# Eight of the convolution's 31 taps as products with diagonal matrices

## The chip, the cores and the metric

One core of a Trainium2 chip runs the kernel. The metric is the device time of one execution in microseconds (us). Engines are named as in the profile: PE is TensorE (PEld its weight loads), DVE is VectorE, ACT is ScalarE, POOL is GpSimd, SP is SyncE, whose queue issues nearly all loads.

## The reference, cut to what matters

A trunk of two layers over 256 tokens of 1024 features. Each layer mixes tokens, then applies a feed-forward block (dense in layer 0, the best two of eight experts in layer 1) and an embedding gate. The part that the change touches is the causal depthwise convolution of the mixer, 31 taps wide, over 512 channels:

```
v = a * jax.nn.sigmoid(gate)
vp = jnp.pad(v, ((0, 0), (CONV_WIDTH - 1, 0), (0, 0)))
y = lax.conv_general_dilated(vp, w_dw[:, None, :], ..., feature_group_count=D_CONV) + b_dw
y = jax.nn.silu(layer_norm(y, g_ln, b_ln));  return y @ w_pw
```

Each channel has its own 31 weights, so with channels on the partitions a tap is "shifted row times one weight per partition, added up". The conv result and the result of a pooling group are concatenated and multiplied by an output projection.

## The kernel before, in words

Everything is float32. Wide products use weights split into a high and a low part in a faster format: three matmuls (L347 high by high, L351 high by low, L352 low by high) for one product. Weights named in `DIRECT` are used whole (L344, L580, L573, L622): such a float32 product is one call in the code and two instructions, each with its own weight load, in the trace. Weight tiles come from one pool of 19 slots; SP issues a load when a slot comes free. ACT casts the high part (L146) and DVE forms the low part (L161).

The engines' orders are written out by hand: `mixer` issues the instructions in program order, and each engine runs its own in that order. The 512 channels are two blocks `b` of two 128-channel columns `i`. For a block, `gate` and `value` project the input (tiles `ps_g`, `ps_v`; each `h` is half of the tokens; 24 instructions for one block and half), ACT takes the sigmoid (L518), DVE multiplies (L523), PE transposes (`turn`, tile `tr`) and a copy puts the result into `vT[b]`, channels on partitions, with room to its left for the shifted reads.

`taps` then emits the taps. With `DT` = 20 and 21 for the two blocks, taps 0 to DT-1 go to DVE (L487 the first, L490 the others, each 128x256, adding into tile `yc`). The other 11 or 10 are made by ACT as products (L492, L495) and summed by POOL into `part` (L498, 128x512). DVE adds `part` to `yc` at the end (L513). The taps of block 0 start when `vT[0]` is there, with the products for block 1 between them: `gate(1,0)`, taps 0 to 4, `value(1,0)`, `gate(1,1)`, more taps, `turn(1,0)`, `value(1,1)`, the remaining taps. Then come the pooling group (`ps_u`, 24 instructions, `turn(1,1)`, 24 more; `ps_d`, `ps_y`), block 1's taps, the first half of the output projection (`ps_o`, L344, four groups of 4 products = 8 instructions, order (c,h) = (0,0), (0,1), (1,0), (1,1)), and the transposes of `yc` (L601, tile `ps_t`), which need all taps. After the third group, by `TS_AT = (1, 0)`, those transposes are put into PE's order. Then follow the layer norm of the conv result (L387 to L609), its transposes (L335), the pointwise product (L622) and the rest of the output projection.

PSUM tiles from `mmt` rotate over four banks, so a tile waits for the reader of the fourth tile before it. In layer 1 the mixer begins while the last input half is still being made: inside `value(0,0)` the function `late` transposes it, ACT casts it (L320, `xH`) and DVE forms its low part (L321, `xL`) for `gate(0,1)`.

Of the kernel before, what the change touches and what calls it, by code (L numbers as in the profile page):

```python
# [9 lines left out]
F32 = mybir.dt.float32  # L10
F32R = mybir.dt.float32r
I32 = mybir.dt.int32
AF = mybir.ActivationFunctionType
ALU = mybir.AluOpType
# [3 lines left out]
P = 128  # L18
D = 1024
S = 256  # L20
# [4 lines left out]
TAPS = 31  # L25
NG = 4
# [8 lines left out]
ND = len(DENSE_CHUNKS)  # L35
SLOTS = 19
HL_START, HL_PRE, HL_FIRST, HL_SECOND, HL_MOE = 8, 12, 8, 6, 10
WO0 = 0
DIRECT = ("pw0", "pw1", "wo00", "wo01")
DT = ((20, 21), (20, 21))  # L40
MORE_AT = 53
NPROD = 8
WARM = 16
WARM1 = 7
GB = 3
# [2 lines left out]
WU_EARLY = 2  # L48
GK = 5
PH = 1  # L50
AHEAD = ((0, 1), (1, 1))
RT = 8
WU_POOL = 3
KP = 5
# [1 line left out]
GL = 6  # L56
END = ((0, 256), (256, 256))
GAINS_AT, PLE_AT = 5, 3
TS_AT = (1, 0)
TEMPS_START, TEMPS_MIX, TEMPS_FFN, TEMPS_MOE, TEMPS_END, TEMPS_GATE = 6, 5, 4, 1, 4, 7  # L60

V_CW, V_CB, V_PS = 0, 124, 128
# [134 lines left out]
def trunk(ctx: ExitStack, tc: tile.TileContext, a: dict, out: bass.AP):  # L197
    nc = tc.nc
# [9 lines left out]
    def acc(name, k=None):  # L208

        if k is None:  # L210
            k = at[0] % 4
            at[0] += 1
        return pacc.tile([P, 512], F32, tag=f"acc{k}", name=name)

    def mmt(name):
        return pmm.tile([P, 512], F32, tag="mm", name=name)

    def tl(tag, shape, dt=F32):
        return ap.tile([P] + shape, dt, tag=tag, name=tag)

    W = Weights(nc, wp)
# [67 lines left out]
    vec = cp.tile([P, L, NV], F32, name="vec")  # L289
# [3 lines left out]
    ident = con[:, C_ID:C_ID + P]  # L293
# [20 lines left out]
    def table(func):  # L314

        nc.scalar.activation(dummy, neghalf, func)
# [25 lines left out]
    def mm(ps, x, it, cols, start, stop):  # L342
        if it["direct"]:
            nc.tensor.matmul(ps, x.f, it["F"][cols], start=start, stop=stop)  # L344
        else:
            wh, wl = it["H"][cols], it["L"][cols]
            nc.tensor.matmul(ps, x.h, wh, start=start, stop=False)  # L347
            if x.l is None:
                nc.tensor.matmul(ps, x.h, wl, start=False, stop=stop)  # L349
            else:  # L350
                nc.tensor.matmul(ps, x.h, wl, start=False, stop=False)  # L351
                nc.tensor.matmul(ps, x.l, wh, start=False, stop=stop)  # L352
# [3 lines left out]
    def proj(ids, ps, x, k0=0, first=True, last=True, free=False, also=None):  # L356

        at = k0
        for n, i in enumerate(ids):
            it = W.get(i)  # L360
            for j in range(it["k"]):
                mm(ps[:, :it["n"]], x[:, at, :], it, (ALL, j), first and n == 0 and j == 0,
                   last and n == len(ids) - 1 and j == it["k"] - 1)
                if also:
                    also(at)
                at += 1
            if free:
                W.done(i)
# [27 lines left out]
    def gains(l, name, n, q=nc.gpsimd, r=None):  # L396
        r = W.temp([2, n]) if r is None else r
        for i, s in enumerate("gb"):
            q.dma_start(r[:, i], a[f"{name}_{s}"][l:l + 1, :].to_broadcast([P, n]))
        return r[:, 0], r[:, 1]  # L400
# [46 lines left out]
    def mixer_loads(l):  # L447

        vs = W.temp([4, 32 + S])
        nc.gpsimd.memset(vs[:, :, 0:32], 0.0)  # L450
        q = nc.sync if l == 0 else nc.gpsimd
        pool = W.temp([16, P])
        mw = pool[:, :12].rearrange("p (a b) t -> p a (b t)", a=NG)
        plw = pool[:, 12:]
        for i in range(2):
            q.dma_start(mw[:, 2 * i:2 * i + 2], a["mw"][i])
        q.dma_start(plw.rearrange("p a b -> p (a b)"), a["w_small"][l, :, 2048:2560])
        cgb = gains(l, "conv_ln", NCONV, q, pd := W.temp([4, NCONV]))
        pd = pd[:, 2:].rearrange("p a (b t) -> p (a b) t", b=2)
        if l == 0:  # L460
            for h in range(2):
                q.dma_start(xr[h], a["x"][h])
        return vs, mw, plw, cgb, pd, W.temp([8, S])

    def mixer(l, xT, xr, late, loads):

        v = [tl(f"s{h}", [512]) for h in range(2)]
        vs, mw, plw, cgb, pd, prod = loads
        vT = [vs[:, 2 * b:2 * b + 2] for b in range(2)]
        yc = tl("yc", [4, S])  # L470
        vb = [[v[h][:, b * 256:(b + 1) * 256] for h in range(2)] for b in range(2)]


        if WO0:
            catP = Split(tl("cat", [NG, S], F32R), prod[:, 4:].bitcast(F32R))
        else:
            catP = Split(None, None, tl("cat", [NG, S]))
        part = [tl(f"gH{b}", [2, S]) for b in range(2)]
        count = [0]

        def tap(b, i, t):
            dt = DT[l][b]
            ct = 2 * b + i
            w1 = vec[:, l, V_CW + ct * TAPS + t:V_CW + ct * TAPS + t + 1]
            src = vT[b][:, i, 2 + t:2 + t + S]
            if t == 0:
                nc.vector.tensor_scalar(yc[:, ct], src, w1, vec[:, l, V_CB + ct:V_CB + ct + 1],  # L487
                                        op0=ALU.mult, op1=ALU.add)
            elif t < dt:
                nc.vector.scalar_tensor_tensor(yc[:, ct], src, w1, yc[:, ct], op0=ALU.mult, op1=ALU.add)  # L490
            elif t == dt:
                nc.scalar.activation(part[b][:, i], src, AF.Copy, scale=w1)  # L492
            else:
                p = prod[:, count[0] % (NPROD // 2) * 2:][:, :2]
                nc.scalar.activation(p[:, i], src, AF.Copy, scale=w1)  # L495
                if i:
                    count[0] += 1
                    nc.gpsimd.tensor_tensor(part[b], part[b], p, op=ALU.add)  # L498

        def taps(b, lo=0, hi=None):  # L500
            dt = DT[l][b]
            hi = hi or dt
            n = TAPS - dt
            by = lambda t: min(n, t * n // dt + (min(t, AHEAD[l][b])))
            for t in range(lo, hi):
                for i in range(2):
                    tap(b, i, t)
                for u_ in range(by(t), by(t + 1)):
                    for i in range(2):
                        tap(b, i, dt + u_)  # L510
            if b and hi == dt:
                for b_ in range(2):
                    nc.vector.tensor_add(yc[:, 2 * b_:2 * b_ + 2], yc[:, 2 * b_:2 * b_ + 2], part[b_])  # L513

        def gate(b, h, between=None):
            pg = acc("ps_g")
            proj(W.names[f"wg{b}{l}"], pg, xT[h], free=h == 1, also=lambda k: k == GB and between and between())
            nc.scalar.activation(vb[b][h], pg[:, :256], AF.Sigmoid)  # L518

        def value(b, h, between=None):  # L520
            pv = acc("ps_v")
            proj(W.names[f"wv{b}{l}"], pv, xT[h], free=h == 1, also=lambda k: k == GB and between and between())
            nc.vector.tensor_mul(vb[b][h], pv[:, :256], vb[b][h])  # L523
# [3 lines left out]
            copy(vT[b][:, :, 32 + h * P:32 + (h + 1) * P], transposes(vb[b][h], 2))  # L527

        W.temps = TEMPS_MIX

        gate(0, 0)
        if l == 0:
# [13 lines left out]
        W.prepare(f"wu{l}", WU_POOL)  # L546
        W.prepare(f"wu{l}", 4, "later")
        taps(0, 0, 5)
        value(1, 0)
        gate(1, 1)  # L550
        taps(0, 5, RT)
# [2 lines left out]
        turn(1, 0)  # L554
        table(AF.Silu)
        value(1, 1)
        taps(0, 12)

        u = [tl(f"g{h}", [512]) for h in range(2)]
        ps = [acc("ps_u") for h in range(2)]  # L560
        ids = W.names[f"wu{l}"]
# [9 lines left out]
        ps = [mmt("ps_d") for g in range(NG)]  # L571
# [6 lines left out]
        for g in range(NG):  # L578
            ps = mmt("ps_y")
            nc.tensor.matmul(ps[:, :S], plw[:, g, :], pd[:, g, :], start=True, stop=True)  # L580
            w = vec[:, l, V_PS + g:V_PS + g + 1]
            nc.scalar.activation((catP.h if WO0 else catP.f)[:, g], ps[:, :S], AF.Copy, scale=w)
            if WO0: nc.vector.scalar_tensor_tensor(catP.l[:, g], ps[:, :S], w, catP.h[:, g].bitcast(F32),
                                           op0=ALU.mult, op1=ALU.subtract)
        taps(1, T1[4])
        W.prepare(f"wo1{l}", None, "later")
        gb = gains(l, "ln1", D, nc.scalar)
# [3 lines left out]
        mix = [[acc("ps_o") for c in range(2)] for h in range(2)]  # L591
        ts = []
        ids = W.names[f"wo0{l}"]
        for c in range(2):
            for h in range(2):
                proj(ids[2 * c:2 * c + 2] if WO0 else ids[c:c + 1], mix[h][c], catP[:, :, h * P:(h + 1) * P], last=False, free=h == 1)
                if (c, h) == TS_AT:
                    for j in range(2):
                        t = mmt("ps_t")
                        for ct in range(4):  # L600
                            nc.tensor.transpose(t[:, ct * P:(ct + 1) * P], yc[:, ct, j * P:(j + 1) * P], ident)  # L601
                        ts.append(t)
# [31 lines left out]
        ps = pointwise(sT[0], lambda: turned(1))  # L634
# [573 lines left out]
    loads = mixer_loads(0)  # L1208
    for l in range(L):
        r = mixer(l, xT, xr, late, loads)  # L1210
        if l % 2 == 0:
            xT, late, ple, loads = dense(l, xr, *r)
# [97 lines left out]
```

## Time and profile before

| what | value |
|---|---|
| time, median of 3 runs (lowest to highest) | 1396.31 us (1393.35 to 1396.6) |
| profiled execution: own time, span | 1394.91 us, 1393.1 us |
| PE busy | 1302.4 us, 93% |
| DVE busy | 1194.2 us, 86% |
| ACT busy | 936.8 us, 67% |
| POOL busy | 92.1 us, of it the sums of taps (L498) 66.1 us in 38 instructions |
| DVE taps L490 | 156 instructions, 91.8 us, mean 660 ns by the grouped page, 467 to 1518 ns each |
| granted PE clock, mean | 0.969 |

The span is from the first to the last instruction; the execution's own time is 1.8 us longer. A busy share is a mean over stages with different limits, so the two mixers (about 31 to 120 us and 345 to 440 us) have to be read by themselves. [...]

### The profile page before, as it was taken

The numbers are of one execution on the slowest core, as the hardware profiler recorded it, in microseconds if no ns is written. First come the engines' busy times: TensorE is split into PE (matmuls) and PEld (weight loads), VectorE is DVE, ScalarE is ACT, GpSimd is POOL, SyncE is SP. The second block draws the span as 40 slices with busy tenths as digits, with TensorE's granted clock in tenths as the row PEclk, the third lists the DMA queues.
The fourth block names the chain that finished last, engine by engine and source line by source line (L and its number), as shares of the span: only waits on it lengthen the run. The fifth ranks groups of instructions, "written<-read, shape, count | busy, mean of one in ns | idle before, by whom it ended". The sixth has DMA issues, their size and how long they took to land. (4 is left out here: it accounts for less than half of the span.)

```text
span 1393.1 us, 16896 instructions
## 1 busy us (share of the span) xinstructions
PE 1302.4 (93%) x6186; PEld 1067.9 (77%) x6186; DVE 1194.2 (86%) x1082; ACT 936.8 (67%) x883; POOL 92.1 (7%) x71
## 2 busy tenths in 40 slices
PE   6769999999868999999999999999999999999777
PEld 5638888888737788878888887788887888888556
DVE  3997844457868698999999999999999999999885
ACT  4543744435444577887888887888888788898652
POOL 0330000001470200000000000000000000000000
PEclk8889999999989899999999999999999999999998
DMA  9334755526545399999999999999999999999850
GB/s 381 129 112 166 264 187 196 192 69 242 219 167 187 109 363 364 421 421 376 403 420 408 400 421 387 390 421 405 400 421 404 376 420 414 388 378 420 353 211 30
DMA packets 62171, 433.08 MB, mean 311 GB/s; under 512 B 6960, under 2 KB 7472, under 8 KB 11008
## 3 DMA queue, kind: packets, MB, share of 16 engines
q1 hardware_dynamic: 60336, 425.60, 77.3%
q0 software_dynamic: 1168, 4.23, 0.9%
q10 hardware_dynamic: 576, 2.10, 0.5%
q8 instruction: 50, 0.82, 0.2%
q14 instruction: 41, 0.34, 0.1%
HBM read 430.85 MB, written 1.05 MB: 310 GB/s over the span
## 5 line engine op out<-in xcount | busy, mean ns | idle before, releaser
L161 DVE TENSOR_TENSOR w<-w 128x2048 fp32r<-128x2048 f32 (+1 forms) x460 | 891.4, 1985 | 53.0 <-ACT w L146 46.7
L146 ACT CAST w<-w 128x2048 fp32r<-128x2048 f32 (+1 forms) x460 | 750.7, 1672 | 134.8 <-PE p L351 42.7
L347 PE MATMUL p<-w,xH 128*128 128x512 f32 (+1 forms) x1096 | 434.0, 396 | 9.0 <-DVEq L1039 6.0
L352 PE MATMUL p<-w,xL 128*128 128x512 f32 (+1 forms) x648 | 250.9, 387 | 1.3 <-DVE xL L321 1.3
L351 PE MATMUL p<-w,xH 128*128 128x512 f32 (+1 forms) x648 | 250.4, 386 | 0.4 <-DVE w L161 0.4
L347 PEld LDWEIGHTS p<-w,xH 128*128 128x128 f32 x1096 | 207.7, 190 | 51.3 <-issue 6.7
L347 PE MATMUL y<-w,gH 128*128 128x512 f32 x448 | 176.2, 393 | 3.0 <-DVE gH L382 2.3
L349 PE MATMUL p<-w,xH 128*128 128x512 f32 x448 | 176.1, 393 | 0.0
L352 PEld LDWEIGHTS p<-w,xL 128*128 128x128 f32 x648 | 122.6, 189 | 26.6 <-DVE xL L321 1.8
L351 PEld LDWEIGHTS p<-w,xH 128*128 128x128 f32 x648 | 122.7, 189 | 24.6 <-DVE w L161 1.3
L347 PEld LDWEIGHTS y<-w,gH 128*128 128x128 f32 x448 | 84.6, 189 | 21.4 <-DVE gH L382 3.0
L349 PEld LDWEIGHTS p<-w,xH 128*128 128x128 f32 x448 | 85.1, 190 | 17.0
L490 DVE SCALAR_TENSOR_TENSOR yc<-w,vec,yc 128x256 f32<-128x256 f32 x156 | 91.8, 660 | 0.0
L349 PE MATMUL y<-w,gH 128*128 128x512 f32 x224 | 88.3, 394 | 1.9 <-DVE w L161 1.9
L352 PE MATMUL y<-w,gL 128*128 128x512 f32 x224 | 87.4, 390 | 1.2 <-DVE gL L321 1.2
L351 PE MATMUL y<-w,gH 128*128 128x512 f32 x224 | 87.3, 390 | 0.0
L498 POOL TENSOR_TENSOR gH<-gH,w 128x512 f32<-128x512 f32 x38 | 66.1, 1738 | 108.5 <-ACT w L495 106.0
L429 POOL DMA_DIRECT2D w<-in_pT x2 | 1.2, 580 | 960.7 <-DVE w L161 802.4
L652 ACT ACTIVATE s<-p 128x512 f32<-128x512 f32 (+1 forms) x69 | 41.1, 598 | 28.0 <-PE p L352 28.0
L321 DVE TENSOR_TENSOR gL<-tr,gH 128x512 fp32r<-128x512 f32 x38 | 25.6, 683 | 32.7 <-ACT gH L320 32.7
L320 ACT CAST gH<-tr 128x512 fp32r<-128x512 f32 x38 | 21.8, 586 | 43.6 <-PE tr L335 43.0
L349 PEld LDWEIGHTS y<-w,gH 128*128 128x128 f32 x224 | 42.5, 190 | 11.0 <-DVE w L161 2.3
(223 smaller groups left out, 1483.3 us busy)
## 6 DMA issues: line engine op xcount, KB each, us to landing
w<-in_exp_w SPq DMA_DIRECT2D x336, 1024.0 KB, 8.8
w<-in_dense_w SPq DMA_DIRECT2D x33, 1024.0 KB, 5.0
w<-in_w_out SPq DMA_DIRECT2D x8, 1024.0 KB, 6.7
w<-in_ple_gate_w SPq DMA_DIRECT2D x8, 1024.0 KB, 5.5
w<-in_w_gv SPq DMA_DIRECT2D x6, 1024.0 KB, 7.3
w<-in_w_u SPq DMA_DIRECT2D x4, 1024.0 KB, 10.2
w<-in_w_gv SPq DMA_DIRECT2D x4, 512.0 KB, 6.7
w<-in_w_small SPq DMA_DIRECT2D x2, 1024.0 KB, 10.5
```

The source lines that it names most:

```text
L146: nc.scalar.copy(h, w)
L161: engine.tensor_tensor(l, w, h.bitcast(F32), op=ALU.subtract)
L320: nc.scalar.copy(dst.h, src)
L321: nc.vector.tensor_sub(dst.l, src, dst.h.bitcast(F32))
L347: nc.tensor.matmul(ps, x.h, wh, start=start, stop=False)
L349: nc.tensor.matmul(ps, x.h, wl, start=False, stop=stop)
L351: nc.tensor.matmul(ps, x.h, wl, start=False, stop=False)
L352: nc.tensor.matmul(ps, x.l, wh, start=False, stop=stop)
L429: nc.gpsimd.dma_start(pT.f, a["pT"][l])
L490: nc.vector.scalar_tensor_tensor(yc[:, ct], src, w1, yc[:, ct], op0=ALU.mult, op1=ALU.add)
L498: nc.gpsimd.tensor_tensor(part[b], part[b], p, op=ALU.add)
L652: nc.scalar.activation(s_[:, :nf], p1[:, :nf], AF.Silu)
```

## The change

Taps 0 to 22 of both blocks go to DVE. Taps 23 to 30 are done on PE: for each of the two columns of a block and each of these taps ACT scales the 128x128 identity by the channel's weights into a diagonal matrix (`dg`, in the slot that held ACT's products before), and PE multiplies it with the shifted `vT`, accumulating 8 products into half of a PSUM bank. DVE adds that bank to `yc` once per block. ACT's products of taps, `part` and POOL's sums are gone. The diagonals of block 0 are made at the mixer's start, those of block 1 after `value(1,1)`. The transposes of `yc` move in front of the third group.

```diff
-DT = ((20, 21), (20, 21))
+DT = 23
-TS_AT = (1, 0)
+TS_AT = (0, 1)
-        return vs, mw, plw, cgb, pd, W.temp([8, S])
+        return vs, mw, plw, cgb, pd, W.temp([16, P])
...
+            if hi is None:
+                y = yc[:, 2 * b:2 * b + 2].rearrange("p a b -> p (a b)")
+                nc.vector.tensor_add(y, y, sums[b])
+        def diagonals(b):
+            for i in range(2):
+                for k in range(TAPS - DT):
+                    nc.scalar.activation(dg[:, i * 8 + k], ident, AF.Copy, scale=weight(2 * b + i, DT + k))
+        def conv(b):
+            sums[b] = mmt("ps_c")
+            for i in range(2):
+                for k in range(TAPS - DT):
+                    nc.tensor.matmul(sums[b][:, i * S:(i + 1) * S], dg[:, i * 8 + k], vT[b][:, i, 2 + DT + k:2 + DT + k + S],
+                                     start=k == 0, stop=k == TAPS - DT - 1)
...
         W.temps = TEMPS_MIX
+        diagonals(0)
         gate(0, 0)
...
         taps(0, 0, 5)
+        conv(0)
         value(1, 0)
...
         value(1, 1)
+        diagonals(1)
         taps(0, 12)
...
+        conv(1)
         taps(1, T1[4])
```

## Rows read from the trace of the kernel before

**Rows 1.** Longest waits of PE, whole span: us in total, times, longest.

```profile
PE ps_t L601 <- DVE yc L513: 23.7, 3, 12.1
PE tr L335 <- DVE s L523: 15.0, 3, 8.4
```

**Rows 2.** DVE in order of time, both mixers: start us, us, line, operation, [idle before].

```profile
40.27 8.29 DVE L490 SCALAR_TENSOR_TENSOR yc<-w,vec,yc 128x256 f32<-128x256 f32 x8
...
52.34 8.42 DVE L490 SCALAR_TENSOR_TENSOR yc<-w,vec,yc 128x256 f32<-128x256 f32 x8
...
61.02 6.41 DVE L490 SCALAR_TENSOR_TENSOR yc<-w,vec,yc 128x256 f32<-128x256 f32 x16
...
68.53 25.05 DVE L490 SCALAR_TENSOR_TENSOR yc<-w,vec,yc 128x256 f32<-128x256 f32 x40
...
358.99 15.57 DVE L490 SCALAR_TENSOR_TENSOR yc<-w,vec,yc 128x256 f32<-128x256 f32 x14
...
410.74 0.69 DVE L513 TENSOR_TENSOR yc<-yc,gH 128x512 f32<-128x512 f32 x1 [11.90 <-POOL gH L498]
```

**Rows 3.** PE in order of time, layer 0's mixer, then two rows of layer 1's.

```profile
34.66 0.28 PE L347 MATMUL ps_v<-w,xH 128*128 128x256 f32 x1
...
48.95 0.48 PE L335 MATMUL tr<-con,s 128*128 128x128 f32 x1 [8.37 <-DVE s L523]
...
54.34 0.40 PE L347 MATMUL ps_u<-w,xH 128*128 128x512 f32 x1
...
59.58 0.39 PE L352 MATMUL ps_u<-w,xL 128*128 128x512 f32 x1
...
66.92 1.89 PE L573 MATMUL ps_d<-w,g 128*128 128x256 f32 x8
68.65 1.05 PE L575 MATMUL ps_d<-w,g 128*128 128x128 f32 x8
...
72.75 10.46 PE L344 MATMUL ps_o<-w,cat 128*128 128x512 f32 x24
...
94.24 2.15 PE L601 MATMUL ps_t<-con,yc 128*128 128x128 f32 x8 [11.02 <-DVE yc L513]
...
100.72 0.60 PE L335 MATMUL tr<-con,s 128*128 128x128 f32 x4
...
355.05 0.28 PE L347 MATMUL ps_v<-w,xH 128*128 128x256 f32 x1
...
417.76 0.49 PE L335 MATMUL tr<-con,s 128*128 128x128 f32 x3
```

**Rows 4.** ACT by shape, whole span (busy us, mean ns of one | idle before); last row: in time.

```profile
L495 ACT ACTIVATE w<-w,vec 128x256 f32<-128x256 f32 x76 | 32.4, 503 | 12.2 <-POOL gH L498 12.2
L568 ACT COPY g<-ps_u 128x512 f32<-128x512 f32 x4 | 2.3, 586 | 23.3 <-PE ps_u L352 23.3
L576 ACT COPY w<-ps_d 128x256 f32<-128x256 f32 x8 | 2.7, 357 | 0.0
...
361.29 3.30 ACT L495 ACTIVATE w<-w,vec 128x256 f32<-128x256 f32 x8
```

**Rows 5.** Start of each mixer, in order of time: ACT in layer 0, then layer 1.

```profile
22.52 0.38 ACT L518 ACTIVATE s<-ps_g 128x256 f32<-128x256 f32 x1 [3.03 <-PE ps_g L352]
...
343.63 1.07 ACT L320 CAST xH<-tr 128x512 fp32r<-128x512 f32 x2
...
345.40 1.28 DVE L321 TENSOR_TENSOR xL<-tr,xH 128x512 fp32r<-128x512 f32 x2
...
346.13 0.39 PE L352 MATMUL ps_g<-w,xL 128*128 128x256 f32 x1 [0.44 <-DVE xL L321]
```

**Rows 6.** Stretches: us, busy (instructions) of PE, PEld, DVE, ACT, POOL; PEclk, DMA share, GB/s.

```profile
374.90:382.20 7.30, 7.25 (x26) 5.99 (x27) 7.19 (x19) 0.59 (x1) 0.00 (x0) 0.77 0.21 53
470.00:480.00 10.00, 9.57 (x41) 7.28 (x40) 9.65 (x19) 7.03 (x4) 6.64 (x2) 1.00 0.01 2
700.00:1300.00 600.00, 590.78 (x2751) 486.81 (x2750) 588.44 (x389) 501.32 (x380) 0.62 (x1) 1.00 1.00 405
```

More of the change, by code (lines that the diff above doesn't have):

```diff
@@ L37 @@
 HL_START, HL_PRE, HL_FIRST, HL_SECOND, HL_MOE = 8, 12, 8, 6, 10
-WO0 = 0
 DIRECT = ("pw0", "pw1", "wo00", "wo01")
-DT = ((20, 21), (20, 21))
+DT = 23
 MORE_AT = 53
-NPROD = 8
 WARM = 16
@@ L50 @@
 PH = 1
-AHEAD = ((0, 1), (1, 1))
 RT = 8
@@ L462, in mixer_loads @@
                 q.dma_start(xr[h], a["x"][h])
-        return vs, mw, plw, cgb, pd, W.temp([8, S])
+        return vs, mw, plw, cgb, pd, W.temp([16, P])
     def mixer(l, xT, xr, late, loads):
         v = [tl(f"s{h}", [512]) for h in range(2)]
-        vs, mw, plw, cgb, pd, prod = loads
+        vs, mw, plw, cgb, pd, dg = loads
         vT = [vs[:, 2 * b:2 * b + 2] for b in range(2)]
@@ L471, in mixer, with weight @@
         vb = [[v[h][:, b * 256:(b + 1) * 256] for h in range(2)] for b in range(2)]
[L474 to L479, printed above, removed]
+        catP = Split(None, None, tl("cat", [NG, S]))
+        sums = [None] * 2
+        def weight(ct, t):
+            return vec[:, l, V_CW + ct * TAPS + t:V_CW + ct * TAPS + t + 1]
@@ L481, in tap @@
         def tap(b, i, t):
-            dt = DT[l][b]
             ct = 2 * b + i
-            w1 = vec[:, l, V_CW + ct * TAPS + t:V_CW + ct * TAPS + t + 1]
             src = vT[b][:, i, 2 + t:2 + t + S]
             if t == 0:
-                nc.vector.tensor_scalar(yc[:, ct], src, w1, vec[:, l, V_CB + ct:V_CB + ct + 1],
+                nc.vector.tensor_scalar(yc[:, ct], src, weight(ct, t), vec[:, l, V_CB + ct:V_CB + ct + 1],
                                         op0=ALU.mult, op1=ALU.add)
[L489 to L492, printed above, removed]
-            else:
[L494 to L498, printed above, removed]
@@ L500, in taps @@
-        def taps(b, lo=0, hi=None):
[L501 to L505, printed above, removed]
+            else:
+                nc.vector.scalar_tensor_tensor(yc[:, ct], src, weight(ct, t), yc[:, ct], op0=ALU.mult, op1=ALU.add)
+        def taps(b, lo=0, hi=None):
+            for t in range(lo, hi or DT):
                 for i in range(2):
                     tap(b, i, t)
[L508 to L513, printed above, removed]
+            if hi is None:
+                y = yc[:, 2 * b:2 * b + 2].rearrange("p a b -> p (a b)")
+                nc.vector.tensor_add(y, y, sums[b])
@@ L581, in mixer @@
             w = vec[:, l, V_PS + g:V_PS + g + 1]
-            nc.scalar.activation((catP.h if WO0 else catP.f)[:, g], ps[:, :S], AF.Copy, scale=w)
-            if WO0: nc.vector.scalar_tensor_tensor(catP.l[:, g], ps[:, :S], w, catP.h[:, g].bitcast(F32),
-                                           op0=ALU.mult, op1=ALU.subtract)
+            nc.scalar.activation(catP.f[:, g], ps[:, :S], AF.Copy, scale=w)
+        conv(1)
         taps(1, T1[4])
@@ L595, in mixer @@
             for h in range(2):
-                proj(ids[2 * c:2 * c + 2] if WO0 else ids[c:c + 1], mix[h][c], catP[:, :, h * P:(h + 1) * P], last=False, free=h == 1)
+                proj(ids[c:c + 1], mix[h][c], catP[:, :, h * P:(h + 1) * P], last=False, free=h == 1)
                 if (c, h) == TS_AT:
```

## The prediction

> **What bounds the kernel now.** I first read the busy shares on the page: PE 93%, DVE 86%. Over the whole span PE is the limit, but that says nothing of the mixers. So next the list of PE's waits: two of the longest stand in the mixer, together 38.7 us [rows 1]. The transposes of `yc` wait three times for the taps, the transposes of `turn` three times for a multiplication on DVE. Third, DVE in order of time, to see why it is late. Sixteen taps took 6.41 us, 0.40 each, where POOL stood still; where POOL summed, eight took 8.29 and 8.42, forty 25.05, fourteen 15.57 [rows 2]. Against 0.40 each that is 5.1 + 5.2 + 9.05 = 19.3 us lost in layer 0 and 10.0 in layer 1. In layer 1 the other side pays too: DVE waited 11.90 us for POOL's last sum [rows 2]. So the mixer is bound by taps on DVE slowed beside POOL, or by POOL itself, while PE stands idle.
>
> **What is removed.** POOL's sums and ACT's products go, and with them the 19.3 and 10.0 us and the 11.90 us wait. ACT's products mostly stood in ACT's idle time; their loss is worth nothing by itself.
>
> **Taps added to DVE.** 92 of the tap instructions per layer where there were 82: 10 x 0.40 = 4.0 us. The add of the sums stays at two per layer.
>
> **Products added to PE.** 16 per block, float32, 128x128 by 128x256, two instructions each: 32. The trace has none with this moving operand (shifted by single elements), but the same shape in `ps_d`: eight start 66.92 to 68.65, 0.216 us each, weights loaded alongside [rows 3]. 32 x 0.216 = 6.92 us per block, 27.7 over the kernel. I take that. The bounds: half of it (the 128-column rows, 8 in 1.05, are the nearest cheaper [rows 3]) and twice it, as at the lower clock (`ps_t`, 8 in 2.15 after a wait, against four transposes in 0.60 [rows 3]).
>
> **Diagonals added to ACT.** A product of 256 columns costs 503 ns, copies of 256 and 512 columns 357 and 586, so a column costs 0.9 ns and 128 columns with a scale 503 - 115 = 388. Eight products in 3.30 us follow each other by 0.40, so overlap hides 0.10 [rows 4]. That leaves 0.29 each, 4.7 us for 16. Bounds: 16 x 0.40 = 6.4 (nothing saved by the smaller width) and 16 x 0.2 = 3.2. Block 1's stand in ACT's wait for `ps_u`: free. Block 0's in layer 0 stand in front of the sigmoid at 22.52, behind an idle 3.03 us [rows 5]: the sigmoid slips by under 2 us, and its multiplication waits for `value(0,0)` anyway: free.
>
> In layer 1 they are not free. There ACT has casts up to the sigmoid that directly precedes the cast of `late` at 343.63. The 16 go in between, so the cast starts near 348.15, `xL` near 348.75 instead of 345.40, and the matmul that waited until 346.13 goes at 349.5 [rows 5]: **3.4 us late**, and all behind it. PE stands idle about as long.
>
> **Clock.** After the 5.4 us wait of layer 1 the stretch ran at a granted 0.77 [rows 6]; after the 8.37 us wait two transposes and 24 matmuls took 54.34 - 48.95 = 5.4 us [rows 3] where full speed gives 3.1, a loss of 2.25. A wait of 3.4 us is shorter than both; I charge 0.8, with bounds 0 and 2.25. [...]
>
> **Layer 0, PE.** The order from 34.66: `conv(0)` 6.92; `value(1,0)` and `gate(1,1)` 5.76 (34.66 to the wait that ended at 48.95, less its 8.37, less 0.16 of the last one's tail); two transposes 0.26; `value(1,1)` 2.88; `ps_u` twice 5.46 (54.34 to 59.58, plus one), transposes 0.26; `ps_d` 2.63 (66.92 to 69.70, less tail); `ps_y` 8 x 0.216 + 0.1 = 1.83; `conv(1)` 6.92; two groups of `ps_o`, 16 x 0.436 (24 in 10.46) = 6.97 [rows 3]. Sum 45.35: PE is at `ps_t` at 80.0. DVE: `ps_t` began at 94.24; less 19.3, plus 4.0, plus 0.6 as the last add now covers the last block, plus 1.2, because after its first ten taps (43.5) it waits for `value(1,0)`, now ready at 34.66 + 6.92 + 2.88 + 0.2 = 44.7. That is 80.7, so PE waits 0.7 instead of 11.02. Then `ps_t` at full clock 1.04 and two groups 6.97: the next transposes start at 88.8 instead of 100.72 [rows 3]. **11.9 us gained.** The norm of the first half (3.2 us on DVE and ACT) hides under those 7 us.
>
> **Layer 1, PE.** 355.05 + 3.4 + 45.35 = 403.8 [rows 3]. DVE here finds its first ten taps done long before `value(1,0)`, which is ready at 368.5; its further taps start at 368.8. Before, they went from 358.99 to 410.74 - 11.90 = 398.84; less 10.0, plus 4.0, plus 0.65 for the second add, 34.5 us [rows 2]: done at 403.3, just in time. Then 1.04 + 6.97: 411.8 instead of 417.76, **6.0 gained, less 0.8 for the clock: 5.1.**
>
> The two `ps_c` tiles each hold one of four PSUM banks until DVE's add. The second `ps_d` waits for the first one's release; that comes at about 61.5 where PE arrives at 62.0. If the taps were slower, this wait would be the first to show.
>
> **Behind the mixers** nothing in the dense block waits for the mixer's engines but through PE, which ran almost without a wait; the gain of layer 0 moves it as a whole. Loads follow slots, which come free with the same instructions, earlier.
>
> **Sum.** 1394.9 of the profiled execution less 17.0 is 1377.9; the median of the runs lies 1.4 above that execution, so 1379.3. I say 1379. A measurement here can tell about 0.3%, 4 us, from no change.
>
> **Rivals.**
> - *Layer 1 returns almost nothing.* The diagonals cost 0.40 each (+1.8), the gap brings the low clock (+1.45) and PE and DVE, now level within a microsecond, miss each other by 2. 1379.3 + 5.1 = 1384. For it: the casts stand wall to wall before 343.63. Against: wide against narrow copies on ACT [rows 4]. 13%.
> - *The gain of layer 1 is given back in the expert stage,* where the DMA share is 1.00 at 405 GB/s [rows 6]. Were the loads there already running at their own pace before the router is done, an earlier mixer would bring nothing: also 1384. Against it: between 470 and 480 us the DMA share is 0.01 [rows 6]; the loads start only when the experts are known, so they move with the mixer. 7%.
> - *The diagonal products are slow and PE becomes the bound: slower than before.* All 128 instructions stand on PE's path, as the sums above show. Each 0.1 us on one costs 12.8 us, so the gain is gone at 0.216 + 17.0/128 = 0.35 us. At 0.43, double, the time is 1379 + 27.7 = 1407. For it: no row has a moving operand that starts at any 4-byte place. Against: DVE reads the same rows at full pace, and `ps_d` has the same shape. 5%.
> - *Taps stay slow without POOL,* so that its sums were not the cause. DVE would be the bound in both mixers by 19 and 10 us, giving about 1408. Against it: all four slow groups, and none of the fast, stand beside POOL's sums. 3%.
>
> **How the numbers follow.** My forecast has 72%, with its own range from 1375 (cheap diagonals, no clock loss) to 1384. The range 1373 to 1388 takes in the first two rivals and leaves out the slow ones. Under 1392 lie the forecast and two rivals, 92%; I take 0.91, as both slow rivals could be milder than priced: 0.04 for no change, 0.05 for slower.
>
> **What would show it.** Right: taps at 0.40 us throughout; 32 instructions of `ps_c` in about 6.9 us; PE's wait at `ps_t` in layer 0 under 2 us; in layer 1 a new PE wait of about 3.4 us for `xH` or `xL`, ended by ACT. Wrong: a pitch of `ps_c` beyond 0.25 us, a PE wait for `dg` or for a `ps_c` bank, or an unchanged start of the layer-1 router against a faster layer 0.

## The result, and the profile after

The changed kernel takes 1376.75 us (median of 4 runs, 1376.11 to 1379.53), against 1396.26 before (also 4 runs). The ratio of the two is put at 0.9876, 95% interval 0.9864 to 0.9888; the medians by themselves divide to 0.986, so 0.1 to 0.2% of it is open. The profiled execution took 1376.18 us, its span is 1374.4. The forecast was 1379.

The busy shares first. POOL falls from 92 to 26 us and PE rises by 15; the mean granted clock, a share of full speed, rises from 0.969 to 0.986. The last line is the group of taps on DVE: 20 more of them than before in 21 us less (70.4 us busy, 478 ns the mean record).

```profile
PE 1317.2 (96%) x6314; PEld 1084.8 (79%) x6314; DVE 1173.5 (85%) x1102; ACT 921.8 (67%) x863; POOL 26.0 (2%) x33
...
L484 DVE SCALAR_TENSOR_TENSOR yc<-w,vec,yc 128x256 f32<-128x256 f32 x176 | 70.4, 478 | 0.0
```

The same stretches of DVE as in [rows 2], changed kernel, layer 0 and then layer 1 (start us, us, line, operation, [idle before]). All groups now run at 0.40 us a tap, counted from one start to the next: 44 in 17.51. A record lasts longer, 478 ns in the mean, since neighbours overlap.

```profile
40.02 3.25 DVE L484 SCALAR_TENSOR_TENSOR yc<-w,vec,yc 128x256 f32<-128x256 f32 x8
44.40 0.42 DVE L514 TENSOR_TENSOR s<-ps_v,s 128x256 f32<-128x256 f32 x1 [1.13 <-PE ps_v L349]
...
62.37 17.51 DVE L484 SCALAR_TENSOR_TENSOR yc<-w,vec,yc 128x256 f32<-128x256 f32 x44
...
357.05 0.42 DVE L514 TENSOR_TENSOR s<-ps_v,s 128x256 f32<-128x256 f32 x1 [6.37 <-PE ps_v L349]
357.39 5.63 DVE L484 SCALAR_TENSOR_TENSOR yc<-w,vec,yc 128x256 f32<-128x256 f32 x14
...
391.58 0.69 DVE L492 TENSOR_TENSOR yc<-yc,ps_c 128x512 f32<-128x512 f32 x1
```

PE in the same stretches, to be held against [rows 3]. The wait at `ps_t` is 0.81 us instead of 11.02 in layer 0, and gone in layer 1, where the longest of before stood, 12.1 [rows 1]. The transposes behind the norm (`tr` at the ends) start at 88.30 instead of 100.72 and at 399.91 instead of 417.76.

```profile
34.41 7.08 PE L503 MATMUL ps_c<-w 128*128 128x256 f32 x32
...
65.75 7.07 PE L503 MATMUL ps_c<-w 128*128 128x256 f32 x32
...
80.72 0.87 PE L594 MATMUL ps_t<-con,yc 128*128 128x128 f32 x6 [0.81 <-DVE yc L492]
88.30 0.60 PE L332 MATMUL tr<-con,s 128*128 128x128 f32 x4
...
346.99 7.08 PE L503 MATMUL ps_c<-w 128*128 128x256 f32 x32
...
392.08 1.12 PE L594 MATMUL ps_t<-con,yc 128*128 128x128 f32 x8
399.91 0.60 PE L332 MATMUL tr<-con,s 128*128 128x128 f32 x4
```

And the place where the change costs something, the start of layer 1's mixer: ACT's 16 diagonals, the casts behind them, and PE, which waits 3.28 us for those casts. It answers to [rows 5].

```profile
330.73 4.79 ACT L497 ACTIVATE w<-con,vec 128x128 f32<-128x128 f32 x16
335.42 0.36 ACT L509 ACTIVATE s<-ps_g 128x256 f32<-128x256 f32 x1
335.69 1.05 ACT L317 CAST xH<-tr 128x512 fp32r<-128x512 f32 x2
...
336.31 0.58 PE L344 MATMUL ps_g<-w,xH 128*128 128x256 f32 x1 [3.28 <-ACT xH L317]
```

### The profile page after: what moved, and what is told of

Its sections match the earlier page's. It is cut to its first block, busy times and chain, and to the rows that moved or that the text cites. A ratio compares the mean times of both kernels' runs of the same rounds, so it can differ in the third digit from the quotient of the medians.

```text
span 1374.4 us, 17077 instructions
## 1 busy us (share of the span) xinstructions
PE 1317.2 (96%) x6314; PEld 1084.8 (79%) x6314; DVE 1173.5 (85%) x1102; ACT 921.8 (67%) x863; POOL 26.0 (2%) x33
## 5 line engine op out<-in xcount | busy, mean ns | idle before, releaser
L344 PEld LDWEIGHTS y<-w,gH 128*128 128x128 f32 x448 | 84.6, 189 | 21.6 <-DVE gH L379 3.1
L484 DVE SCALAR_TENSOR_TENSOR yc<-w,vec,yc 128x256 f32<-128x256 f32 x176 | 70.4, 478 | 0.0
L346 PEld LDWEIGHTS y<-w,gH 128*128 128x128 f32 x224 | 42.6, 190 | 11.0 <-DVE w L158 2.3
L349 PEld LDWEIGHTS y<-w,gL 128*128 128x128 f32 x224 | 42.0, 188 | 10.4 <-DVE gL L318 1.6
L348 PEld LDWEIGHTS y<-w,gH 128*128 128x128 f32 x224 | 42.1, 188 | 9.0
```

The lines of the kernel that those rows point to most:

```text
L484: nc.vector.scalar_tensor_tensor(yc[:, ct], src, weight(ct, t), yc[:, ct], op0=ALU.mult, op1=ALU.add)
```

## The experiments

All ratios are to the kernel before, timed beside each version on the same chip, with 95% intervals. The chips differ from version to version, so versions are compared with each other by these ratios and by their traces. A layer's "stretch" is, for layer 0, the time from its first `ps_v` to the transposes behind the norm, and for layer 1 the time from its first `ps_g` to those transposes. In the changed kernel these are 62.9 us (25.36 to 88.30) and 73.7 (326.25 to 399.91).

**Was POOL what slowed the taps?** The kernel before without its sums:

```diff
                 if i:
                     count[0] += 1
-                    nc.gpsimd.tensor_tensor(part[b], part[b], p, op=ALU.add)
```

> The kernel before, with POOL's 38 sums of taps left out (ACT still makes the products; 9 or 10 of the taps of a block are missing from the output). Theory, POOL's sums slow the taps on DVE: all taps at 0.40 us, DVE 19.3 us earlier in layer 0 and 10.0 us in layer 1, the 11.9 us wait for POOL gone; PE then comes level with DVE and the time falls by about 42 us, to some 1354. Rival, ACT's products or DVE itself slow the taps: the slow groups stay, only the 11.9 us wait goes, about 1384.

Measured: 1350.03 us, ratio 0.9688 (0.9663 to 0.9713), 43.9 us under the 1393.94 of the kernel before in the same runs. The group of all taps, then the forty of layer 0 and the fourteen of layer 1:

```profile
L490 DVE SCALAR_TENSOR_TENSOR yc<-w,vec,yc 128x256 f32<-128x256 f32 x156 | 62.5, 476 | 0.0
```
```profile
57.88 15.92 DVE L490 SCALAR_TENSOR_TENSOR yc<-w,vec,yc 128x256 f32<-128x256 f32 x40
...
337.69 5.62 DVE L490 SCALAR_TENSOR_TENSOR yc<-w,vec,yc 128x256 f32<-128x256 f32 x14
```

The forty of layer 0 took 25.05 us beside the sums and take 15.92 without them, the fourteen of layer 1 took 15.57 and take 5.62 [rows 2]. ACT's products are still made, so they do not slow the taps. This run also shows what the mixers would take if ten taps per block cost nothing but ACT's time, with 20 or 21 left on DVE.

**Is dropping POOL the whole gain?** All 31 taps on DVE, nothing on PE or POOL (from the changed kernel; the diagonals, the products and the add of their sums are taken out, the last not shown):

```diff
-DT = 23
+DT = 31
-TS_AT = (0, 1)
+TS_AT = (1, 0)
...
-        diagonals(0)
-        conv(0)
-        diagonals(1)
-        conv(1)
```

> All 31 taps on DVE, no products on ACT, none on PE, nothing on POOL; transposes of yc after the third group as before. Theory, dropping POOL only repays what the extra taps cost, and the gain came from giving taps to PE's idle time: DVE loses 19.3 and 10.0 us of slowing and gains 42 taps x 0.40 = 16.8 us in each layer, less the adds: layer 0 about 3 us earlier, layer 1 about 6 us, so about 1387. Rival, dropping POOL is the whole of the gain: about 1377, as the changed kernel.

Measured: 1384.41 us, ratio 0.9929 (0.9906 to 0.9951). That is 9.5 us under the 1393.94 of the kernel before in the same runs, where about 9 were expected. PE's longest wait is back at the transposes, 8.7 us in each layer:

```profile
PE ps_t L587 <- DVE yc L484: 17.4, 2, 8.7
```

So POOL's ten or eleven taps per block were worth so little that DVE alone does better; the rest of the gain (0.9929 to 0.9876, about 7 us; 6.7 by the spans of 1381.1 and 1374.4) needs the products on PE. It comes from layer 0 alone, which the total hides: there the stretch is 70.8 us here (25.06 to 95.89) and 62.9 in the changed kernel, but in layer 1 it is 72.2 (333.92 to 406.12) and 73.7. In layer 1 the change, as it stands, is a little worse than dropping POOL; what the diagonals cost there is asked by the experiment after the next.

**Does PE have any slack left?** Each diagonal product twice:

```diff
-                    nc.tensor.matmul(sums[b]..., start=k == 0, stop=k == TAPS - DT - 1)
+                    for r in range(2):
+                        nc.tensor.matmul(sums[b]..., start=k == 0 and r == 0, stop=k == TAPS - DT - 1 and r == 1)
```

> The changed kernel with each diagonal product issued twice (these taps count double in the output): 128 more instructions on PE. Theory, PE's order has no slack left in either mixer: 128 x 0.216 = 27.7 us more, less the 0.8 us wait of layer 0, about 1403.6. Rival, the products fill idle time of PE while DVE sets the end: under 10 us more.

Measured: 1402.39 us, ratio 1.0059 (1.004 to 1.0077), 25.6 us above the changed kernel's median; by the spans (1400.6 and 1374.4) 26.2, where 26.9 were expected. The 128 more instructions have the duration of the first 128:

```profile
L504 PE MATMUL ps_c<-w x256: 377/378/381, 34.0 to 411.3; 128*128 128x256 f32 x128
```

All but about 1 us of PE's added work is paid. The run also shows how the rival "slower than before" would have come out.

**What do layer 1's first diagonals cost?** Emitted behind the casts of the late half:

```diff
-        diagonals(0)
+        if l == 0:
+            diagonals(0)
         gate(0, 0)
...
             value(0, 0, late)
+            diagonals(0)
             gate(0, 1)
```

> The changed kernel with layer 1's first 16 diagonals emitted behind the casts of the late input half instead of in front of them. Theory: they stood in PE's path for 4.4 us (3.3 us of wait and the low clock behind it), so 1376.7 - 4.4 = 1372.3, and PE's wait for xH falls back to the 0.4 us of before. Rival, DVE's taps set layer 1's end and the delay was hidden: 1376.7.

Measured: 1372.76 us, ratio 0.9848 (0.9824 to 0.9872); the medians differ by 4.0 from the changed kernel's, though the intervals overlap. The trace decides. The stretch from layer 1's first `ps_g` to the transposes behind the norm is 69.3 us (325.86 to 395.13) instead of 73.7 (326.25 to 399.91): the expected 4.4. Now layer 1 is also 2.9 us under the 72.2 with all taps on DVE. PE's wait is the one of before:

```profile
333.31 0.39 PE L349 MATMUL ps_g<-w,xL 128*128 128x256 f32 x1 [0.44 <-DVE xL L318]
```

**Are DVE's waits for `value(1,0)` on the path?** The first block's products behind `gate(1,1)`:

```diff
-        conv(0)
         value(1, 0)
         gate(1, 1)
+        conv(0)
```

> The changed kernel with conv(0) behind gate(1,1) instead of in front of value(1,0). DVE's waits of 1.1 us (layer 0) and 6.4 us (layer 1) for value(1,0) go, PE's work is the same. Theory, PE sets both mixers' ends: only PE's 0.8 us wait at the transposes of layer 0 goes, about 0.8 us in all, hardly to be measured. Rival, DVE's taps set the end of layer 1's mixer: about 6 us faster.

Measured: 1377.44 us, ratio 0.9866 (0.9851 to 0.9881): no difference that can be told from the changed kernel. In layer 0 the wait did go, and the stretch is 62.0 us instead of 62.9, as the theory has it. In layer 1 the run does not test the rival, which I had not seen: DVE's wait only moved on to the next multiplication, still 6.47 us, because that one's `value(1,1)` now stands behind the products. The stretch is 74.1 us there instead of 73.7; the 0.4 more is the clock behind the casts (see the fourth point of the next section).

```profile
350.56 0.42 DVE L514 TENSOR_TENSOR s<-ps_v,s 128x256 f32<-128x256 f32 x1
...
362.99 0.42 DVE L514 TENSOR_TENSOR s<-ps_v,s 128x256 f32<-128x256 f32 x1 [6.47 <-PE ps_v L349]
```

Both of these edits together:

> The later conv(0) and the later diagonals of layer 1 together: 4.4 + 0.8 = 5.2 us under the changed kernel. PE waits for nothing in either mixer between the two; DVE arrives at layer 1's transposes about 7 us early. Rival, with PE 4.4 us earlier DVE becomes the bound again: under 4 us.

Measured: 1370.81 us, ratio 0.9829 (0.9814 to 0.9844). Layer 1's stretch is 69.3 us as with the late diagonals alone, and layer 0 is 1 us shorter than in the changed kernel. The total is as expected, 5.2 us by the spans (1374.4 and 1369.2); "7 us early" for DVE was wrong: its last add ends at 387.2, and `ps_t` starts at 387.03, its first two transposes needing only block 0.

**Two taps back to DVE in layer 1.** The next one rests on the same mistaken 7 us; it was set down before either had run (`DT = (23, 25)`, both edits kept):

> As a_both, and in layer 1 two more taps per block go back to DVE (25 there, 6 on PE): PE loses 16 instructions per block, 32 x 0.216 = 6.9 us less half of... in numbers: 2 taps x 2 columns x 2 blocks x 0.433 = 3.5 us less on PE, DVE 8 taps x 0.40 = 3.2 us more, which its 7 us of slack hold. Theory: 3.5 us under a_both, about 8.7 under the changed kernel. Rival, DVE's slack isn't there: no gain over a_both.

Measured: 1374.35 us, ratio 0.9851 (0.9838 to 0.9865), 3.5 us above the version it came from. The two intervals touch, but layer 1's stretch is 72.1 us instead of 69.3. The forecast failed, and the rival held: DVE's slack was not there, and PE waits for it:

```profile
PE ps_t L596 <- DVE yc L492: 4.8, 1, 4.8
```

**The wait really removed.** In layer 1 the products go behind `value(1,1)`, in layer 0 they stay behind `gate(1,1)`:

```diff
         gate(1, 1)
-        conv(0)
+        if l == 0:
+            conv(0)
...
         value(1, 1)
+        if l:
+            conv(0)
```

> As a_best (late diagonals in layer 1, 25 taps on DVE there), but in layer 1 conv(0) goes behind value(1,1), so that DVE waits for neither multiplication; in layer 0 it stays behind gate(1,1), since there PE would wait 3.3 us for DVE without it. Theory, DVE's 6.5 us only moved from the wait for value(1,0) to the wait for value(1,1): now they are really free, DVE and PE both reach layer 1's transposes some 3.4 us before a_both, so about 1367.4. Rival, the taps on DVE are slower or later for another reason: PE waits some 5 us at the transposes again, about 1374.

Measured: 1368.71 us, ratio 0.9816 (0.9803 to 0.9829), the lowest time of a version that does all the work, though its interval overlaps that of the two edits alone. DVE's second multiplication waits no more, and the transposes start without a wait of PE:

```profile
350.42 0.41 DVE L514 TENSOR_TENSOR s<-ps_v,s 128x256 f32<-128x256 f32 x1
...
382.21 0.69 DVE L492 TENSOR_TENSOR yc<-yc,ps_c 128x512 f32<-128x512 f32 x1
```
```profile
382.60 1.24 PE L599 MATMUL ps_t<-con,yc 128*128 128x128 f32 x8
390.54 0.60 PE L332 MATMUL tr<-con,s 128*128 128x128 f32 x4
```

Layer 1's stretch is 66.0 us (324.58 to 390.54), 3.3 less than with the two edits alone, where 3.4 were expected, and 6.2 less than the 72.1 of the version with the moved wait. The total fell by only about 2, since what follows took 2 us longer than in the run with the two edits alone (976.4 against 974.4 us to the end of the span). Part of it may be the router's stage, where 14 us ran at a granted 0.52 here (420 to 434) and 0.63 there (424 to 438); why, no run shows.

**Is the earlier place of the transposes worth anything?** The changed kernel with `TS_AT = (1, 0)`:

> The changed kernel with the transposes of yc after the third group of the output projection, as before the change (TS_AT = (1, 0)). Theory, the move by itself is worth nothing: PE's 0.8 us wait in layer 0 is covered by the third group, and one group of 3.5 us still covers the norm (2.5 us on DVE, 0.6 on ACT, behind the first bank of transposes), so within 1 us of the changed kernel. Rival, the norm comes out from under the one group: up to 3.5 us slower in each layer.

Measured: 1376.29 us, ratio 0.9865 (0.985 to 0.988): nothing that the times can tell, as expected. The traces say a little more: with the later place layer 0's stretch is 61.9 us instead of 62.9, since PE's 0.81 us wait is gone, and layer 1's is 73.7 in both. So the earlier place gains nothing and costs layer 0 about 1 us.

## Why the prediction was right

The mechanism held step by step; one reading of the rows was wrong, without harm to the forecast.

- *POOL slows the taps.* Right, and shown by the run without sums. Taps at 0.40 everywhere; the last add of layer 0 ends at 80.7 where 80.7 was worked out. One reading was wrong: that none of the fast groups stands beside POOL's sums. Forty taps of layer 1 ran at 0.40 beside the first of nine sums (last section); there that sum took 15.27 us instead, and the 11.90 us wait of DVE was the price. The forecast took that wait off as well, so nothing hung on it.
- *Products at 0.216 us.* Right: 32 in 7.08 us with the last one's tail, (7.08 - 0.38)/31 = 0.216. That is the pitch of `ps_d` [rows 3], so the shifted start of the moving operand costs nothing here. All 128 lie on the path, as the doubled run shows. No wait for `dg` or for a `ps_c` bank appears in PE's list.
- *Diagonals 4.7 us.* 4.79 measured, free in layer 0 (the sigmoid behind them slipped from 22.52 to 24.66, 0.6 of it from before the diagonals, and nobody waited) and in ACT's wait for `ps_u`.
- *3.4 us late in layer 1, 0.8 for the clock.* Together 4.2, and 4.4 measured. Counted from layer 1's first `ps_g` (338.69 before, 326.25 after), the matmul that waits for `xL` starts 10.78 us on instead of 7.44: 3.3 late. From there to the first `ps_v` behind it PE took 3.8 us (337.03 to 340.81) instead of 2.7 (346.13 [rows 5] to 348.87): the clock cost 1.0. The lines are one of before, then the changed kernel's two, then the stretch, at a granted 0.67:

```profile
348.87 0.28 PE L347 MATMUL ps_v<-w,xH 128*128 128x256 f32 x1
```
```profile
337.03 0.58 PE L349 MATMUL ps_g<-w,xL 128*128 128x256 f32 x1
...
340.81 0.28 PE L344 MATMUL ps_v<-w,xH 128*128 128x256 f32 x1
```
```profile
336.30:341.00 4.70, 4.69 (x26) 4.47 (x27) 1.61 (x3) 0.43 (x1) 0.00 (x0) 0.67 0.37 101
```

  The late diagonals gave all 4.4 us back. But the length of the wait does not settle when the clock falls. In the changed kernel and with the doubled products the matmuls behind this wait of 3.28 us soon follow each other by 0.21 us, in the changed kernel at a granted 0.50 (336.30 to 338.10). With the later `conv(0)`, behind the same 3.28 us, they start at 1.00, most of them 0.12 us apart, and fall to 0.50, 0.21 apart, only after 1.8 us, and the clock cost 1.5:

```profile
335.80:337.60 1.80, 1.56 (x10) 1.35 (x11) 1.62 (x3) 0.45 (x1) 0.00 (x0) 1.00 0.49 205
337.60:340.80 3.20, 3.20 (x17) 3.20 (x16) 0.00 (x0) 0.00 (x0) 0.00 (x0) 0.50 0.49 125
```

  So behind the same wait two of these three traces have the low clock at once and one does not; what decides it, no run shows. The upper bound of 2.25 us, read behind a wait of 8.37 us [rows 3] and the source of the first rival's 1.45 (2.25 less 0.8), was too high for all three: the clock cost 1.0, 1.1 (349.42 to 353.28 with the doubled products) and 1.5. My 0.8, an estimate, was a little low.
- *Layer 0 gains 11.9.* 12.4 measured; 0.25 of it was there before `conv(0)` started (34.41 instead of 34.66), and 0.4 is that two of the eight transposes were done before the wait (79.53), where the working had all eight behind it.
- *The dense block moves as a whole.* From the transposes behind the norm to layer 1's first `ps_g`: 238.0 us before (100.72 to 338.69), 238.0 after (88.30 to 326.25).
- *Layer 1 gains 5.1.* 5.4 measured (79.1 to 73.7 us). PE reached `ps_t` with DVE level with it, as worked out (392.08, with DVE's last add ending at 392.27). That this is less than dropping POOL alone gives (79.1 to 72.2) the prediction did not say.
- *Nothing is given back in the expert stage.* From layer 1's transposes to the end 975.3 us before, 974.5 after; over the other kernels here it lies between 973.5 and 976.4, so the 0.8 lies within the scatter.

Sum: 12.4, 5.4 and 0.8 make the 18.7 by which the spans differ; 17.0 were forecast. Of the 1.7 between them 0.5 is layer 0, 0.3 layer 1 and 0.8 scatter. The clock, the term most off in size, was off by 0.2.

## What to carry to other kernels

An engine that "helps" can cost more than it does (here all taps on DVE took 9.5 us less than with POOL's help): take its work out in one run and compare the engine beside it, before balancing shares between them. When two engines have been brought level, an instruction in front of a cast in one engine's order can decide a layer (here 4.4 us, more than the products gained in that layer), so ask of each inserted block who waits behind it, and compare layer by layer. And a wait that an edit removes has to be looked up at the next instruction of that engine too: here it moved on by one multiplication, and a version that counted on it lost 3.5 us.

## What the runs showed of the hardware that was not expected

The loss between DVE and POOL goes either way. In layer 0, and in the first block of layer 1, the taps beside the sums were slowed, to 0.63 to 1.11 us each in the mean of a group [rows 2]. In the second block of layer 1 of the kernel before, forty taps ran at full pace, 0.40 us each, and POOL's nine sums took 26.01 us, one of them 15.27, where the median of all 38 is 1.33 (the third line gives shortest, median and longest in ns). DVE's taps and the add behind them end at 398.84; ACT, which waits for the first of those sums, goes on at 399.99.

```profile
384.69 26.01 POOL L498 TENSOR_TENSOR gH<-gH,w 128x512 f32<-128x512 f32 x9 [10.81 <-ACT w L495]
...
382.32 15.92 DVE L490 SCALAR_TENSOR_TENSOR yc<-w,vec,yc 128x256 f32<-128x256 f32 x40
...
L498 POOL TENSOR_TENSOR gH<-gH,w x38: 1262/1334/15270, 40.7 to 409.4; 128x512 f32<-128x512 f32 x38
```

The first of the nine sums starts at 384.69, and the forty taps run from 382.32 to 398.24. Each tap is an instruction of its own, and yet one sum lasted 15.27 us beside an unbroken run of them. Why, and what decides which of the two engines loses, no run here shows, only the times.
